# A, B and C heads of a hybrid encoder: TensorE's order written out, C keys loaded a triple ahead, value and bias loads from GpSimd's queue

## The chip, the cores and the metric

The kernel runs on one core of a Trainium2 chip. A core has five engines that work in parallel, each with its own instruction stream: PE (TensorE, matrix multiplies and transposes into PSUM), DVE (VectorE), ACT (ScalarE), POOL (GpSimd) and SP (SyncE, which here does nothing but start DMAs). An engine runs its instructions strictly in the order in which they stand, and an instruction that waits for a semaphore holds up all that stand behind it. DMAs that are started from SP, ACT or POOL stand in that engine's order too. The metric is the device time of one execution in microseconds (us).

## The reference

The program is a two-layer encoder trunk on 2048 tokens of width 1024. Four groups of attention heads run side by side on one projected input, and their outputs, each multiplied by a gate, are joined and projected back:

```python
for l in range(DEPTH):                      # DEPTH = 2
    h = _rmsnorm(x, norm_g[l])
    z = jnp.einsum('bsd,de->bse', h, w_in[l])
    (q_a, k_a, v_a, g_a, q_b, k_b, v_b, g_b,
     q_c, k_c, v_c, g_c, q_d, k_d, v_d, g_d) = jnp.split(z, offs, axis=-1)
    ...
    o_a = _dense_blocked(q_a, k_a, ...)      # A: 4 query heads, 2 key heads, all 2048 keys
    o_b = _window_sink(q_b, k_b, ...)        # B: keys within 128 of the query, with a sink logit
    o_c = _neighbourhood(q_c, k_c, v_c, rpb_c[l], sc_hd)   # C: 8 x 16 neighbours on a grid of 32 x 64, with a bias
    o_d = _diff_blocked(q_d, k_d, ...)       # D: difference of two softmaxes
    mix = jnp.concatenate([o_a * jax.nn.silu(g_a), o_b * jax.nn.silu(g_b),
                           o_c * jax.nn.silu(g_c), o_d * jax.nn.silu(g_d)], axis=-1)
    x = x + jnp.einsum('bsm,md->bsd', mix, w_out[l])
return _rmsnorm(x, final_g)
```

## The kernel before

The kernel is written in Python as a sequence of tile operations. A framework (`TileContext` with `schedule_with_timeline_sim=True`) then places each engine's instructions: it simulates the program and takes, for each engine, the operation that its simulation finds ready first, so the order in which an engine runs its work need not be that in which the code was written. Tiles come from pools with a fixed number of buffers; a new tile waits until the readers of the buffer's earlier tile are done.

A layer has four stages: the first part of the input projection (lines L319 to L323, tiles z), the D heads with the rest of the projection beside them, the phase of the A, B and C heads, and the output projection (L222, tiles y). The change lies in the third. In layer 0 it runs from about 1070 to 1692 us, in layer 1 from about 2880 to 3530 us.

The third stage is made of 96 *units* in 32 *triples*. A triple is one A unit (two query heads that share a key head, one block of 128 queries, all 2048 keys) and two small units: for the first 16 triples B units (first key head of A, `ps` 0), for the last 16 C units (second key head of A, `ps` 1). `drive` writes the work of a triple in this order:

- 12 slots. In each slot stands one *front* of the current triple: four PE transposes of probabilities into a PSUM tile PTp (L513 for A, L530 for B and C), which ACT or DVE (every third) copies out to P or PT (`evac`, L474 and L472). Behind it stands one score step of the next triple: two matmuls into S (L496), Sb (L999) or Sc (L1036), which DVE reduces to maxima while it copies them out (L497, L1001, L1037). ACT takes the exponentials (L504 for A).
- then the *backs*, the products of the probabilities with the values: 16 matmuls into O for the A unit (L519, `dense_back`), and into Obc, one PSUM tile for both small units, for B or C (L538, `small_back`). fp32 matmuls show up as two passes in the profile. Before, the backs go through their blocks downwards, and through the units of the triple from last to first.
- then the *finishes* (`fin_plain`), which run within the first three slots of the next triple: the first step copies each unit's output to an SBUF tile os (L567 to L570 for A with ACT and DVE, L572 for B and C with ACT), and POOL multiplies the gate by the reciprocal sum into gg (L543). Two slots later (`finish2`) PE transposes gg into the upper half of O or Obc (L548: O<-idr,gg, Obc<-idr,gg), DVE multiplies it by os into mix (L551) or mixc (L558), and a DMA stores that in mx. The os and gg tiles come from the pool `ov`, which has two buffers for each.

`prep(ps, t + 1)` runs when the scores of unit t start. It loads the queries (q, L963) and, in some triples, keys: `k_batch` loads a block of 512 keys of the A, B or C heads into kl (L947; pool `ql`, one buffer), transposes them on PE into kT (L98) and splits them in two terms (L954, L956) into the long key tiles kA, kB, kC. These, and the value tiles vc of the C heads, share a pool `big` of ten buffers, so that a vc tile takes the buffer of a key tile that is done. `load_vc` fills a vc tile with 6 to 8 DMAs (L940), `load_bias` a bias tile (bedge, bint) with a memset and four DMAs (L148, L152). SP starts nearly all DMAs: gates gt (L614, L616), q, kl, vc, bias, mx and the output weights wos (L254).

## Time and profile before

| | us |
|---|---|
| median of 3 runs | 3717.33 |
| lowest and highest run | 3710.25, 3719.14 |
| the profiled execution, its time | 3713.1 |
| the profiled execution, its span | 3711.3 |
| PE busy | 3516.1 (95%) |
| DVE busy | 2492.1 (67%) |
| ACT busy | 2095.2 (56%) |
| POOL busy | 944.4 (25%) |

The span is the stretch from the first to the last recorded instruction of the profiled execution; its time has 1.8 us around it. Rows of a timeline read: start in us, duration in us, engine, line, operation, output<-inputs, number of instructions that the row joins, and in brackets how long the engine had been idle and what ended that. SPq stands for the DMA starts on SP's queue, PE for matmuls, PEld for weight loads (they overlap with PE). Rows of waits read: engine, tile and line that waited <- what it waited for: us in total, times, longest. Rows of a stretch read: from:to, length, then busy time and count of PE, PEld, DVE, ACT, POOL, then the granted TensorE clock (1.00 is full speed), the busy share of the DMA engines and GB/s.

### The profile page before, as it was taken

How to read it: one execution, taken by the hardware profiler on the slowest of the kernel's cores; microseconds unless marked ns; L12 is line 12 of the kernel's file. 1: busy time of each engine (PE TensorE's matmuls, PEld its weight loads, DVE VectorE, ACT ScalarE, POOL GpSimd, SP SyncE). 2: the span in 40 equal slices, each digit the busy share in tenths (PEclk: the TensorE clock that was granted, in tenths of full speed). 3: DMA queues.
4: the chain of work that ended last, by engine and by line, in shares of the span. 5: the costliest groups of instructions: out<-in, count | busy, mean ns of one | idle time of the engine just before them, and what ended most of it. 6: DMA issues, size and time to landing. Idle time of an engine off the chain costs nothing.

```text
span 3711.3 us, 71694 instructions
## 1 busy us (share of the span) xinstructions
PE 3516.1 (95%) x25232; PEld 2967.4 (80%) x25232; DVE 2492.1 (67%) x7829; ACT 2095.2 (56%) x3961; POOL 944.4 (25%) x1604
## 2 busy tenths in 40 slices
PE   8989999999989788999999899999999897899999
PEld 8979898888957666777899798989888676677787
DVE  4377878778777665774233778787877776667733
ACT  4345656556657565772143556565666676667721
POOL 4455324533100000001034553254321000000000
PEclk9999999999999998999999999999999899999999
DMA  4532225332133323325345323252232323343243
GB/s 142 191 100 83 80 76 172 86 83 83 59 98 86 89 83 107 93 78 181 132 129 192 98 78 86 78 182 73 78 84 73 90 81 92 88 117 89 87 151 119
DMA packets 353867, 386.44 MB, mean 104 GB/s; under 512 B 58914, under 2 KB 296674, under 8 KB 348386
## 3 DMA queue, kind: packets, MB, share of 16 engines
q1 hardware_dynamic: 349186, 366.11, 33.4%
q10 hardware_dynamic: 4320, 15.73, 1.2%
q8 instruction: 200, 3.28, 0.4%
q14 instruction: 161, 1.32, 0.1%
HBM read 258.83 MB, written 122.86 MB: 103 GB/s over the span
## 4 chain that ended last, share of the span: by engine, by line
PE 76%; DVE 7%; DMA 5%; POOL 4%; ACT 3%; issue 3%; SPq 2%; POOLq 0%; DVEq 0%; ACTq 0%
PE O L519 11%; PE S L496 10%; PE PTp L513 10%; PE y L222 10%; PE z L319 9%; PE z L321 9%; PE z L323 9%; DVE P L497 3%; PE PTp L530 2%; PE Obc L538 2%; ACT P L504 2%; PE Sc L1036 2%; SPq L940 1%; DMA wst<-in_w_in_dram 1%; DVE wt L313 1%
## 5 line engine op out<-in xcount | busy, mean ns | idle before, releaser
L497 DVE TENSOR_SCALAR_CACHE_REDUCE P<-S 128x512 f32<-128x512 f32 x1536 | 1017.7, 686 | 255.6 <-PE S L496 166.2
L319 PE MATMUL z<-wt,ht 128*128 128x256 f32 (+1 forms) x3008 | 891.3, 297 | 19.8 <-POOL wt L312 10.4
L321 PE MATMUL z<-wt,ht 128*128 128x256 f32 (+1 forms) x3008 | 882.9, 294 | 2.6 <-DVE wt L313 2.6
L323 PE MATMUL z<-wt,ht 128*128 128x256 f32 (+1 forms) x3008 | 882.3, 294 | 0.0
L513 PE MATMUL PTp<-idr,P 128*128 128x128 f32 x4096 | 624.6, 278 | 19.4 <-ACT P L474 10.3
L474 ACT COPY P<-PTp 128x512 f32<-128x512 f32 x864 | 491.3, 583 | 217.1 <-PE PTp L513 210.4
L319 PEld LDWEIGHTS z<-wt,ht 128*128 128x128 f32 x3008 | 568.8, 189 | 38.8 <-POOL wt L312 12.5
L504 ACT ACTIVATE P<-P,nm 128x2048 f32<-128x2048 f32 x256 | 513.9, 2008 | 144.4 <-DVE jk L503 139.9
L321 PEld LDWEIGHTS z<-wt,ht 128*128 128x128 f32 x3008 | 569.0, 189 | 16.1 <-DVE wt L313 4.6
L513 PEld LDWEIGHTS PTp<-idr,P 128*128 128x128 f32 x4096 | 491.5, 143 | 111.0 <-issue 23.6
L323 PEld LDWEIGHTS z<-wt,ht 128*128 128x128 f32 x3008 | 569.1, 189 | 8.4 <-issue 0.8
L496 PE MATMUL S<-kA,q 128*128 128x512 f32 x1024 | 348.1, 435 | 0.3
L543 POOL TENSOR_TENSOR gg<-gt,rzh 128x128 f32<-128x128 f32 x192 | 78.8, 411 | 1016.1 <-PE O L548 578.4
L222 PE MATMUL y<-wot,ms 128*128 128x512 f32 x1440 | 332.9, 393 | 3.4 <-ACT ms L211 2.0
L222 PEld LDWEIGHTS y<-wot,ms 128*128 128x128 f32 x1440 | 271.9, 189 | 64.2 <-ACT ms L211 2.4
L720 DVE SCALAR_TENSOR_TENSOR P<-P,cf,P 128x2048 f32<-128x2048 f32 x128 | 306.4, 2394 | 2.5
L312 POOL TENSOR_SCALAR wt<-wst,g 128x256 fp32r<-128x256 f32 (+1 forms) x336 | 208.2, 631 | 390.0 <-PE z L323 290.8
L504 ACT ACTIVATE P<-P,nm,rr_a 128x2048 f32<-128x2048 f32 x128 | 268.8, 2100 | 62.6 <-DVE jk L503 61.8
L519 PE MATMUL O<-P,vA 128*64 128x256 f32 x2048 | 272.6, 392 | 0.0
L519 PE MATMUL O<-P,vd 128*64 128x256 f32 x2048 | 240.9, 388 | 1.6 <-ACT P L474 1.6
L313 DVE SCALAR_TENSOR_TENSOR wt<-wst,g,wt 128x256 fp32r<-128x256 f32 (+1 forms) x344 | 195.3, 596 | 44.2 <-POOL wt L312 40.5
L496 PE MATMUL S<-kdt,qd 128*128 128x512 f32 x512 | 214.6, 442 | 8.3 <-DVE P L497 5.8
(195 smaller groups left out, 5130.6 us busy)
## 6 DMA issues: line engine op xcount, KB each, us to landing
wst<-in_w_in_dram SPq DMA_DIRECT2D x320, 128.0 KB
qd<-qd SPq DMA_DIRECT2D x128, 128.0 KB
htd<-ht SPq DMA_DIRECT2D x16, 1024.0 KB
ht<-htd SPq DMA_DIRECT2D x16, 1024.0 KB
q<-qsA SPq DMA_DIRECT2D x128, 128.0 KB
q<-qsB SPq DMA_DIRECT2D x64, 256.0 KB
q<-qc SPq DMA_DIRECT2D x64, 256.0 KB
mload<-mx ACTq DMA_DIRECT2D x30, 512.0 KB
```

The lines of the kernel that those rows point to most:

```text
L222: PE.matmul(ys[c], lhsT=ms[:, a, kc], rhs=wts[k][:, b, c * 512:(c + 1) * 512], start=(k == 0 and i == 0), stop=(k == KD - 1 and i == 2))
L313: V.scalar_tensor_tensor(wt[:, 1, :], s, g8[:, k:k + 1], wt[:, 0, :].bitcast(F32), op0=ALU.mult, op1=ALU.subtract)
L319: PE.matmul(z, lhsT=h[:, 0, kc], rhs=wk[:, 0, :], start=(k == 0), stop=False)
L321: PE.matmul(z, lhsT=h[:, 0, kc], rhs=wk[:, 1, :], start=False, stop=False)
L323: PE.matmul(z, lhsT=h[:, 1, kc], rhs=wk[:, 0, :], start=False, stop=(k == KD - 1))
L474: A.copy(dst, src)
L496: PE.matmul(s, lhsT=q, rhs=k_ap[:, c:c + 512], start=(i == 0), stop=(i == len(q_list) - 1))
L497: V.tensor_scalar(p[:, c:c + 512], s, 1.0, None, op0=ALU.mult, op1=ALU.max, accum_out=mx[:, j:j + 1])
L504: A.activation(p, p, ACTF.Exp, bias=nm, scale=scale, accum_out=zacc)
L513: PE.transpose(tp[:, (h * 2 + a) * 128:(h * 2 + a + 1) * 128], p[:, h, j * 128:(j + 1) * 128], idn)
L519: PE.matmul(u["o"][a * 64:(a + 1) * 64, 0:256], lhsT=u["v"](0, j), rhs=u["p"][:, :, j * 128:(j + 1) * 128], start=(j >= NT - 2), stop=(j < 2))
L720: V.scalar_tensor_tensor(p0, p1, cf, p0, op0=ALU.mult, op1=ALU.add)
```

## The change

It has four parts.

1. The `drive` of the A, B and C heads stands in `tc.manual_schedule` for PE: within it PE's instructions are issued in the order in which the code is written. The other engines are still placed by the simulation.
2. The backs of a triple are written as A, first small unit, second small unit, and their blocks upwards (`fixed`; the D heads keep the downward order).
3. `k_batch` is split. `k_load` starts the DMA of the keys at one `prep`, `k_build` transposes and splits them at the next; `ql` has two buffers. The first B block is still loaded and built at once.
4. The DMAs of `load_vc` and `load_bias` are started from POOL's queue (`nc.gpsimd`): in both layers 120 for vc and 48 for bias.

Lines after the first edit move: L543 is L544 after, L548 is L549, L513 stays, L538 is L539, L940 is L941, L947 is L948, L963 is L970, L1036 is L1043.

```diff
--- before.py
+++ after.py
@@ -149,7 +149,7 @@
         for r in range(4):
             i0 = min(max(4 * rg + r - 4, 0), 24) - w0
             row = w0 + i0 - 4 * rg - r + 7
-            nc.sync.dma_start(out=dst[r * 32:r * 32 + 32, :, i0 * 40:i0 * 40 + 320],
+            nc.gpsimd.dma_start(out=dst[r * 32:r * 32 + 32, :, i0 * 40:i0 * 40 + 320],
                               in_=rep_d[l][ch][:, :, row * 40:row * 40 + 320])
 
     ht = {}
@@ -514,10 +514,11 @@
                 evac(p[:, :, c], tp.rearrange("p (h k) -> p h k", h=2), u["ev"])
 
             def dense_back(u):
-                for j in reversed(range(NT)):
+                js = range(NT) if u["fixed"] else range(NT - 1, -1, -1)
+                for n, j in enumerate(js):
                     a = j % 2
                     PE.matmul(u["o"][a * 64:(a + 1) * 64, 0:256], lhsT=u["v"](0, j), rhs=u["p"][:, :, j * 128:(j + 1) * 128],
-                              start=(j >= NT - 2), stop=(j < 2))
+                              start=(n < 2), stop=(n >= NT - 2))
 
             def small_front(u, i):
                 ws, n, kw = u["ws"], u["n"], u.get("kw", 128)
@@ -533,10 +534,10 @@
 
             def small_back(u):
                 n, kw = u["n"], u.get("kw", 128)
-                for j in reversed(range(n)):
+                for j in range(n):
                     for h in range(2):
                         PE.matmul(u["o"][h * 64:(h + 1) * 64, u["oc"]:u["oc"] + 128], lhsT=u["v"](h, j),
-                                  rhs=u["pt"][0:kw, (j * 2 + h) * 128:(j * 2 + h + 1) * 128], start=(j == n - 1), stop=(j == 0))
+                                  rhs=u["pt"][0:kw, (j * 2 + h) * 128:(j * 2 + h + 1) * 128], start=(j == 0), stop=(j == n - 1))
 
             def finish(gt, coef):
                 gg = ov.tile([128, 2, 64], F32, tag="gg", name="gg")
@@ -683,7 +684,7 @@
                     flush()
                     for u in g:
                         u["get_o"](u)
-                    for u in reversed(g):
+                    for u in g:
                         u["back"](u)
                     for u in g:
                         fins.append(u["fin"](u))
@@ -909,7 +910,7 @@
                             return kds[kv, c]
                         return f
                     units = [dict(kv=kv, t=t, k=get_kd(kv), qp=dv, s=d_scores, par=True, ns=16, nv=8, ev=0, fin=fin_d, fb=6 + kv,
-                                  p1=p1p, front=dense_front, back=dense_back, get_o=own_o,
+                                  p1=p1p, fixed=False, front=dense_front, back=dense_back, get_o=own_o,
                                   v=lambda h, j, kv=kv: vd[:, j, kv * 64:(kv + 1) * 64]) for kv in range(2) for t in range(NT)]
 
                     for u in units:
@@ -937,14 +938,20 @@
                     for j in range(nr // 3):
                         k0 = (w0 + 3 * j) * 64 + 24 * ch
                         src = bass.AP(tensor=vc_d.tensor, offset=vc_d.offset + k0 * 256, ap=[[16384, 3], [256, 40], [1, 256]])
-                        nc.sync.dma_start(out=v[0:120, ch, j, :], in_=src)
+                        nc.gpsimd.dma_start(out=v[0:120, ch, j, :], in_=src)
                 return v
 
-            def k_batch(ql, g, b):
-                c = slice(b * 512, (b + 1) * 512)
+            def k_load(ql, g, b):
+                kls = []
                 for pr in range(2 if g == "C" else 1):
                     kl = ql.tile([128, 4, 128], F32R, tag="kl", name="kl")
                     nc.sync.dma_start(out=kl.bitcast(F32), in_=ks_d[g, b][:, :, pr * 128:(pr + 1) * 128])
+                    kls.append(kl)
+                return kls
+
+            def k_build(g, b, kls):
+                c = slice(b * 512, (b + 1) * 512)
+                for pr, kl in enumerate(kls):
                     p = tps.tile([128, 512], F32, tag="t", name="kT")
                     for i in range(4):
                         transpose_raw(p[:, i * 128:(i + 1) * 128], kl[:, i, :])
@@ -1051,7 +1058,7 @@
 
             def a_unit(kv, t, q, pre):
                 return dict(kv=kv, t=t, s=a_scores, par=True, ev=EVA1 if kv else EV3, ns=8, nv=8, fin=fin_plain, fb=kv, q=q, pre=pre,
-                            front=dense_front, back=dense_back, get_o=own_o, oc=0,
+                            front=dense_front, back=dense_back, get_o=own_o, oc=0, fixed=True,
                             v=lambda h, j: vt["A"][:, j, kv * 64:(kv + 1) * 64])
 
             def pair_o(u):
@@ -1065,7 +1072,7 @@
                 return dict(kv=i, t=t, s=sc, par=False, ev=EVC if sc is c_scores else EVB, ns=ns, nv=nv, fin=fin_plain, fb=fb, q=q, pp=px, bias=bias, pre=pre,
                             front=small_front, back=small_back, get_o=pair_o, oc=128 * i, ptp=ptp)
 
-            with tc.tile_pool(name="qst", bufs=2, reuse_waits="tile") as qst, tc.tile_pool(name="ql", bufs=1, reuse_waits="tile") as ql, \
+            with tc.tile_pool(name="qst", bufs=2, reuse_waits="tile") as qst, tc.tile_pool(name="ql", bufs=2, reuse_waits="tile") as ql, \
                     tc.tile_pool(name="cb", bufs=1, reuse_waits="tile") as cb, tc.tile_pool(name="px", bufs=4, reuse_waits="tile") as px, \
                     tc.tile_pool(name="pt", bufs=2, reuse_waits="tile") as ptp, \
                     tc.tile_pool(name="ops2", bufs=1, space=PSUM, reuse_waits="tile") as ops2, \
@@ -1073,22 +1080,28 @@
                 tpool = cycle([tps, tps, tps3])
                 load_v("A")
                 kt["B"] = [big.tile([128, S], F32R, tag="b", name=f"kB{i}") for i in range(2)]
-                k_batch(ql, "B", 0)
+                k_build("B", 0, k_load(ql, "B", 0))
                 load_v("B")
+                loaded = []
                 bint = [None, cb.tile([128, 4, 480], F32, name="bint1")]
                 cc_ = {}
                 cm = {"pool": cb}
                 qq = {}
 
                 def prep(ps, t):
+                    while loaded:
+                        k_build(*loaded.pop(0))
                     if t < NT:
                         g = "BC"[ps]
+                        nk = None
                         if ps == 0 and t % 4 == 2 and t < 14:
-                            k_batch(ql, "B", t // 4 + 1)
+                            nk = "B", t // 4 + 1
                         if ps == 0 and t == 4:
                             kt["A"].append(big.tile([128, S], F32R, tag="b", name="kA1"))
                         if ps == 0 and 4 <= t < 8:
-                            k_batch(ql, "A", t - 4)
+                            loaded.append(("A", t - 4, k_load(ql, "A", t - 4)))
+                        if nk:
+                            loaded.append((*nk, k_load(ql, *nk)))
                         if ps == 1 and t == 2:
                             bint[0] = big2.tile([128, 4, 512], F32, tag="b", name="bint0")[:, :, 0:480]
                             load_bias(l, bint[0], 3, 0)
@@ -1096,7 +1109,7 @@
                             load_bias(l, bint[1], 3, 1)
                             kt["C"] = [big.tile([128, S], F32R, tag="b", name=f"kC{i}") for i in range(4)]
                         if ps == 0 and t >= 12:
-                            k_batch(ql, "C", t - 12)
+                            loaded.append(("C", t - 12, k_load(ql, "C", t - 12)))
                         qq["A", ps, t] = q_batch(qst, "A", t, 2 * ps, 2)
                         qq[g, ps, t] = q_batch(qst, g, t, 0, 4)
                     elif ps == 0:
@@ -1131,7 +1144,8 @@
                             if k == MS0:
                                 ms_first.append(load_split(mx_d[0].rearrange("p a b -> p (a b)"), dv, "qd"))
                             wo_tiles.append(load_split(w_out[l, k * 128:(k + 1) * 128, :], dv, "qd"))
-                drive([units[i:i + 3] for i in range(0, len(units), 3)], GAP3, iter(()), 0, ex3)
+                with tc.manual_schedule(engines={mybir.EngineType.PE}):
+                    drive([units[i:i + 3] for i in range(0, len(units), 3)], GAP3, iter(()), 0, ex3)
 
         dvx.close()
         prev_mx = mx_d
```

On PE, in the third B triple of layer 1, the finishing transposes (O<-idr,gg of the A unit, Obc<-idr,gg of the two B units) stood like this among scores S and Sb and fronts PTp before:

```order
L548 MATMUL O<-idr,gg 128x128
L496 MATMUL S<-kA_35899,q 128x512 x2
L513 MATMUL PTp<-idr,P 128x128 x4
L496 MATMUL S<-kA_35899,q 128x512 x4
L513 MATMUL PTp<-idr,P 128x128 x4
L548 MATMUL Obc<-idr,gg 128x128
L513 MATMUL PTp<-idr,P 128x128 x8
L496 MATMUL S<-kA_35899,q 128x512 x4
L999 MATMUL Sb<-kB_38469,q 128x384
L1000 MATMUL Sb<-kB_38469,q 128x384
L513 MATMUL PTp<-idr,P 128x128 x4
L548 MATMUL Obc<-idr,gg 128x128
```

and so after:

```order
L496 MATMUL S<-kA_35902,q 128x512 x2
L513 MATMUL PTp<-idr,P 128x128 x4
L496 MATMUL S<-kA_35902,q 128x512 x2
L513 MATMUL PTp<-idr,P 128x128 x4
L549 MATMUL O<-idr,gg 128x128
L549 MATMUL Obc<-idr,gg 128x128 x2
L496 MATMUL S<-kA_35902,q 128x512 x2
L513 MATMUL PTp<-idr,P 128x128 x4
```

The three transposes that lay apart, with four score steps and more between the first and the last, stand next to each other, and fronts and scores alternate one by one.

On POOL, in the phase of layer 0, the gates gg stood alone but for the memsets of the bias tiles before:

```order
L543 TENSOR_TENSOR gg<-gt,rzh 128x128 x47
L148 MEMSET bedge 128x1440
L148 MEMSET bint_18895 128x4x480
L543 TENSOR_TENSOR gg<-gt,rzh 128x128 x3
L148 MEMSET bedge 128x1440
```

and after they stand with the vc loads among them (gg x33 is eleven triples):

```order
L544 TENSOR_TENSOR gg<-gt,rzh 128x128 x33
L941 DMA vc<-vc_211 120x1x256 x14
L544 TENSOR_TENSOR gg<-gt,rzh 128x128 x11
L941 DMA vc<-vc_211 120x1x256 x22
L544 TENSOR_TENSOR gg<-gt,rzh 128x128
```

22 of them stand between the second and the third gg of the fifteenth triple. Later in the phase, runs of 8, 8 and 6 stand between the second and the third gg of three C triples.

On SP, around the load of the second block of C keys (kl<-ksC_1) in layer 0, before:

```order
L963 DMA q<-qsB_13_162 64x1024
L616 DMA gt<-gsB_11_206 128x128
L552 DMA mx_9_230<-mix 128x128
L963 DMA q<-qsB_13_162 64x1024
L940 DMA vc<-vc_211 120x1x256 x11
L947 DMA kl<-ksC_1_174 128x4x128
L616 DMA gt<-gsA_12_191 128x128
```

and after:

```order
L553 DMA mx_9_230<-mix 128x128
L617 DMA gt<-gsB_11_206 128x128
L970 DMA q<-qsA_14_147 64x512 x2
L970 DMA q<-qsB_13_162 64x1024 x2
L948 DMA kl<-ksC_1_174 128x4x128 x2
L617 DMA gt<-gsA_12_191 128x128
```

The eleven vc loads that stood directly ahead of the keys are gone from SP, and both halves of the block are loaded one behind the other.

## The prediction

> **What bounds the kernel now.** I read the page first, then the busy time of each engine in the two A/B/C phases, then TensorE's waits there, and last the timelines around the waits. PE is the bound of the whole program:

> ```profile
> span 3711.3 us, 71694 instructions
> PE 3516.1 (95%) x25232; PEld 2967.4 (80%) x25232; DVE 2492.1 (67%) x7829; ACT 2095.2 (56%) x3961; POOL 944.4 (25%) x1604
> ```

> The profiled execution took 3713.1 us, 4.2 below the median 3717.33 and inside the three runs' 3710.25 to 3719.14. 0.3%, about 11 us, is what a measurement of this kernel can tell from no change. The change touches only the phase of the A, B and C heads, which is the stretch from 1070 to 1692 us in layer 0 and from 2880 to 3530 us in layer 1. These four rows give each engine's busy time there, and the granted clock:

> ```profile
> 1070.00:1370.00 300.00, 269.46 (x2022) 203.64 (x2020) 214.35 (x813) 203.55 (x441) 19.73 (x48) 0.95 0.30 82
> 1370.00:1692.00 322.00, 297.70 (x2278) 222.35 (x2277) 215.19 (x746) 209.17 (x412) 26.60 (x55) 0.96 0.33 94
> 2880.00:3190.00 310.00, 274.80 (x1992) 203.79 (x1991) 226.07 (x831) 210.09 (x433) 20.22 (x48) 0.95 0.31 85
> 3190.00:3530.00 340.00, 323.77 (x2488) 241.59 (x2488) 233.84 (x819) 228.50 (x459) 28.91 (x61) 0.98 0.35 99
> ```

> PE is busy 1165.7 of 1272 us: no more than 106 us can come from filling its gaps. The largest wait of PE, first of layer 0, then of layer 1 (in total, times, longest):

> ```profile
> PE kT L98 <- DMA kl<-ksC: 19.4, 3, 18.1
> ...
> PE kT L98 <- DMA kl<-ksC: 18.8, 3, 17.9
> ```

> So 38 us of the gaps are two stalls on C keys, and they have a visible cause: on SP's queue the load of these keys (L947) stands behind eleven vc loads.

> ```profile
> 1271.55 19.29 SPq L940 DMA_DIRECT2D vc<-vc  x11
> 1290.95 1.58 SPq L947 DMA_DIRECT2D kl<-ksC  x1
> 1299.41 0.75 PE L98 MATMUL kT<-idr,kl 128*128 128x128 f32 x4 [18.13 <-DMA kl<-ksC]
> ```

> **Part 1: written order and early keys, the gain.** I measure a triple by the start of its first finishing transpose (O<-idr,gg): 32 in each layer, 31 intervals.

> ```profile
> 1113.59 0.27 PE L548 MATMUL O<-idr,gg 128*128 128x128 f32 x1
> 1180.19 0.27 PE L548 MATMUL O<-idr,gg 128*128 128x128 f32 x1
> 1195.70 0.27 PE L548 MATMUL O<-idr,gg 128*128 128x128 f32 x1
> 1318.59 0.27 PE L548 MATMUL O<-idr,gg 128*128 128x128 f32 x1
> 1338.06 0.27 PE L548 MATMUL O<-idr,gg 128*128 128x128 f32 x1
> 1501.74 0.27 PE L548 MATMUL O<-idr,gg 128*128 128x128 f32 x1
> 1518.63 0.27 PE L548 MATMUL O<-idr,gg 128*128 128x128 f32 x1
> 1679.62 0.27 PE L548 MATMUL O<-idr,gg 128*128 128x128 f32 x1
> 1692.08 0.30 PE L548 MATMUL O<-idr,gg 128*128 128x128 f32 x1 [1.28 <-DVE os L570]
> 2959.54 0.27 PE L548 MATMUL O<-idr,gg 128*128 128x128 f32 x1
> 3524.41 0.30 PE L548 MATMUL O<-idr,gg 128*128 128x128 f32 x1 [0.70 <-DVE os L570]
> ```

> The 31 intervals last 578.5 us in layer 0 and 564.9 in layer 1. An undisturbed B triple takes 15.51 (1180.19 to 1195.70), a C triple 16.89 (1501.74 to 1518.63, with no gap on PE), a B triple that also builds C keys 19.47, the last interval 12.46. In written order every triple has the same plain alternation, so I give each its undisturbed length: 15 x 15.51 + 15 x 16.89 + 12.46 = 498.5, plus 4 x 3.96 for C keys, plus 7 other key builds at 0.4 (half of the 0.75 us above, where the clock was 0.50) = 517.1 per layer. The gain is 61.4 + 47.8 = 109.2 us. It holds the two key stalls, the small waits and the piecemeal order of the late C triples; taking the backs as A, B, B and in ascending order, the second ql buffer and the loads a triple ahead are in it and cost nothing more (the same matmuls; SP has fewer DMAs ahead of the keys). If small waits of the ACT kind survive, up to 20 of it fails.

> **Part 2: the finishing chain, the loss.** The three finishing transposes of a triple stand apart in the order before, with scores of later slots between. In written order they are neighbours. Each hangs on the last: the third os copy on ACT writes the buffer that mix of the first transpose frees on DVE; Obc's first transpose writes the tile that this copy reads; Obc's second needs the mixc that follows the first. Before, the same chain runs with cover:

> ```profile
> 1501.77 0.71 PE L496 MATMUL S<-kA,q 128*128 128x512 f32 x2
> 1502.09 0.40 POOL L543 TENSOR_TENSOR gg<-gt,rzh 128x128 f32<-128x128 f32 x1 [9.99 <-DMA q<-qsA]
> 1502.84 0.29 DVE L551 TENSOR_TENSOR mix<-O,os 128x128 f32<-128x128 f32 x1
> 1503.43 0.27 ACT L572 COPY os<-Obc 128x128 f32<-128x128 f32 x1
> 1505.46 0.27 PE L548 MATMUL Obc<-idr,gg 128*128 128x128 f32 x1
> 1506.27 0.29 DVE L558 TENSOR_TENSOR mixc<-Obc,os 128x128 f32<-128x128 f32 x1
> 1508.24 0.27 PE L548 MATMUL Obc<-idr,gg 128*128 128x128 f32 x1
> ```

> It took 6.5 us, 1501.74 to 1508.24, and none of it was idle on PE. Now PE stands still for it, since it issues in order. Its hand-overs, where nothing else is in the way, are short:

> ```profile
> 1693.18 0.29 DVE L551 TENSOR_TENSOR mix<-O,os 128x128 f32<-128x128 f32 x1
> 1693.51 0.27 ACT L572 COPY os<-Obc 128x128 f32<-128x128 f32 x1 [0.92 <-DVE mix L551]
> 1323.08 0.56 ACT L474 COPY P<-PTp 128x512 f32<-128x512 f32 x1
> 1323.70 0.66 PE L530 MATMUL PTp<-idr,Pb 128*128 128x128 f32 x4 [1.13 <-ACT P L474]
> ```

> From the first transpose at 0: mix starts at 1.10 (1502.84 - 1501.74; DVE has the same score and probability copies ahead of it) and ends at 1.39, the copy starts 0.04 later and ends at 1.70, PE 0.06 after that at 1.76; 0.35 to the next engine (POOL's gg 1502.09 after 1501.74) gives mixc at 2.11 to 2.40, and the third transpose at 2.46. A transpose alone delays the next matmul by 0.03 (1501.77), so the net loss is 2.46 - 2 x 0.03 = 2.40 us. The ends: 1.0 if the chain were half covered, which the waits as built do not allow but a fast DVE would approach (without the 0.75 us in which DVE is behind it is 1.65), and 3.0 if another ACT copy (0.56) stands in the way. I take 2.40, since the DVE queue ahead of mix is that of the rows. 62 triples x 2.40 = 148.8 us. Behind the waiting transpose stand the scores S, and DVE, ACT and the next triple wait for them.

> **Part 3: the clock.** A stall of this size also slows what follows it:

> ```profile
> 1100.00:1103.40 3.40, 1.53 (x12) 1.00 0.78 189
> 1103.40:1106.90 3.50, 3.50 (x18) 0.51 0.06 14
> ```

> PE was busy 1.53 of 3.40 us, and the next 3.5 us ran at 0.51. That costs half of 3.4, 1.7 us. A stall that idles PE for some 1.9 us leaves a 3.4 us window under half busy only when nearly all of it falls into that window, for (3.4 - 2.4)/3.4 = 0.3 of the triples. 62/3 x 1.7 = 35 us; the ends are 0 and 105 (every triple). [...]

> **Part 4: vc and bias loads on POOL.** 120 vc and 48 bias DMAs leave SP for POOL's queue, where gg (L543) runs, and gg feeds the chain. In the new order 22 vc loads stand ahead of the third gg of one B triple of each layer, and 8, 8 and 6 ahead of that of three C triples. What one costs POOL no row shows; the nearest are SP's own:

> ```profile
> L940 SPq DMA_DIRECT2D vc<-vc x120: 681/750/2484, 1266.4 to 3356.8; - x120
> 1516.45 4.90 SPq L940 DMA_DIRECT2D vc<-vc x5
> 1512.71 1.95 PE L519 MATMUL O<-P,vA 128*64 128x256 f32 x16
> 1514.48 1.92 PE L538 MATMUL Obc<-PT,vc 120*64 120x128 f32 x32
> 1516.33 0.66 PE L513 MATMUL PTp<-idr,P 128*128 128x128 f32 x4
> ```

> The cover: the 8 wait for the last Obc of the old buffer, which ends at 1516.33, 2.30 before the first transpose; with the chain's 2.46 that is 4.76 us. The 22 wait first for the last S on the old A keys, which ends four score slots, O's back and a B back earlier: slots of 0.92 (two and a half of them in the 2.30), a back of two times 1.77 (1512.71 to 1514.48) and 24 of the 32 passes that take 1.85 (1514.48 to 1516.33): 3.7 + 3.5 + 1.4 + 4.8 = 13.4 us. At the 0.98 us of the run of five (4.90/5) the stalls are 22 x 0.98 + 0.40 (the gg itself) - 13.4 = 8.6, twice 8 x 0.98 + 0.40 - 4.76 = 3.5, and 1.5: 17.1 per layer, 34.2 in all. At the median 0.75 it is 14; at the 1.75 of the run of eleven 102; at the longest, 2.48, 166; at a gg's 0.40 nothing. I take 0.98, the price with the queue not choked. The 14 vc loads ahead of another triple's first gg have a whole triple to run in (14 x 0.98 = 13.7 of 15.51), and the bias loads, 4 at a time, fit in the cover. Moving them off SP gains nothing beyond part 1.

> [...]

> **Sum.** 3713.1 - 109.2 + 148.8 + 35.1 + 34.2 = 3822.0 us, 2.9% above the profiled execution and 2.8% above the median.

> **Rivals.**
> - *Faster.* The chain costs less than 109.2/62 = 1.76 us a triple, nothing else grows. For it: 1.65 if DVE reaches mix at once. Against it: in the steady triple DVE is not there at once. At 1.0 us, no clock loss and 14 for POOL: 3713 - 109 + 62 + 14 = 3680.
> - *About unchanged.* 1.65 a triple and no clock loss: 3713 - 109 + 102 + 14 = 3720.
> - *Worse: DVE's work holds POOL's issue up.* Each vc load then costs POOL 1.75 to 2.48 us (the run of eleven, the longest row) and PE waits for gg: 102 to 166 in place of 34, 3890 to 3954. For it: gg and 22 loads in one queue, and DVE is busy 70% of this phase (889 of 1272 us in the four rows). [...]
> - *The change doesn't do what it says.* The key stalls come back, because the loads still stand on SP's one queue behind loads that wait for buffers: 38 us of the gain fail, 3860. Against: no vc load stands ahead of a kl load on SP any more.

> **Chances.** The sum's case 0.56 (its own range 3755 to 3885, from chains of 1.8 to 2.7 us and a clock loss of 0 to 60), faster 0.23, about unchanged 0.07, worse 0.10, stalls back 0.04. The range, 3680 to 3925, cuts a third of the faster case and half of the worse. Faster by over 0.3%: 0.23; within: 0.07; slower: 0.70.

> **What would show it.** Right: in the new trace, Obc's transposes wait on ACT os and on DVE mixc in nearly each triple, together about 2 us; kT waits on kl are gone; intervals of 17.9 for B and 19.3 for C triples; a granted clock under 0.95 in these phases; gg late behind vc loads in four triples a layer. Wrong: no such waits and B triples near 15.5, or POOL's DMA rows under 0.5 us with the clock at 1.00.

## The result, and the profile after

The changed kernel takes 3816.02 us (median of 4 runs, 3813.22 to 3819.26) against 3718.23 (4 runs, 3710.25 to 3726.55): the ratio is 1.0263, 95% interval 1.0239 to 1.0287, so it is 2.6% slower. The forecast was 3822, with a range of 3680 to 3925.

The head of the page after, span and PE:

```profile
span 3811.3 us, 71858 instructions
PE 3522.4 (92%) x25232; PEld 3021.1 (79%) x25232; DVE 2521.7 (66%) x7829; ACT 2097.8 (55%) x3961; POOL 1056.8 (28%) x1772
```

PE is as busy as before (3516.1) and the span is 100 us longer, so at first sight all of the loss is idle time of PE. The busy time by stretch says where it is. The stretches run from the first O<-idr,gg of a layer to the last; these are the two of before (columns as in the prediction):

```profile
1113.59:1692.08 578.49, 529.67 (x4059) 399.51 (x4057) 401.14 (x1445) 385.99 (x795) 43.38 (x97) 0.96 0.32 91
2959.54:3524.41 564.87, 525.99 (x4058) 395.78 (x4057) 401.00 (x1444) 385.88 (x795) 43.26 (x97) 0.98 0.33 93
```

and these the two of after:

```profile
1116.00:1743.41 627.41, 538.26 (x4088) 427.90 (x4087) 420.49 (x1457) 390.11 (x800) 94.84 (x173) 0.93 0.33 84
3001.11:3624.88 623.77, 536.60 (x4087) 427.51 (x4086) 420.87 (x1456) 390.06 (x799) 94.91 (x173) 0.93 0.33 84
```

The phases grew by 48.9 and 58.9 us, 107.8 together; the stage between them got 9.8 shorter. PE's idle time went from 87.7 to 176.3 us, its busy time up by 19, at a lower clock. What PE waits for in the two phases after, layer 0 first:

```profile
PE Obc L549 <- ACT os L573: 50.1, 31, 2.8
PE Obc L549 <- POOL gg L544: 20.1, 29, 2.8
PE O L549 <- DVE os L571: 6.2, 2, 5.1
...
PE Obc L549 <- ACT os L573: 48.0, 31, 2.5
PE Obc L549 <- POOL gg L544: 27.8, 29, 11.1
```

The four rows of Obc are 146 us in 120 waits, all at the second and third finishing transpose. No wait for kl is left. One steady C triple, in the timelines of PE, DVE, ACT and POOL, shows the chain:

```profile
1562.66 0.27 PE L549 MATMUL O<-idr,gg 128*128 128x128 f32 x1
1563.75 0.29 DVE L552 TENSOR_TENSOR mix<-O,os 128x128 f32<-128x128 f32 x1
1564.08 0.27 ACT L573 COPY os<-Obc 128x128 f32<-128x128 f32 x1 [1.53 <-DVE mix L552]
1564.49 0.30 PE L549 MATMUL Obc<-idr,gg 128*128 128x128 f32 x1 [1.56 <-ACT os L573]
1564.83 0.29 DVE L559 TENSOR_TENSOR mixc<-Obc,os 128x128 f32<-128x128 f32 x1 [0.78 <-PE Obc L549]
1564.87 0.40 POOL L544 TENSOR_TENSOR gg<-gt,rzh 128x128 f32<-128x128 f32 x1 [1.46 <-PE Obc L549]
1565.26 0.30 PE L549 MATMUL Obc<-idr,gg 128*128 128x128 f32 x1 [0.47 <-POOL gg L544]
1565.32 0.71 PE L496 MATMUL S<-kA,q 128*128 128x512 f32 x2
```

From the first transpose: mix at 1.09, the copy at 1.42, the second transpose at 1.83, mixc at 2.17, the third transpose at 2.60, the next score at 2.66. The next such transpose comes at 1581.60, an interval of 18.94 us.

The view puts the last 0.47 us down to gg, but it was mixc that the third transpose waited for. This gg ends at 1565.27, after the transpose has started (1565.26); mixc ends at 1565.12, 0.14 before it, the same 0.14 that lie between the end of the os copy (1564.35) and the second transpose, and so it is in all 54 triples without a late gg. The transpose's own gg was made at 1563.01, in the buffer that the first transpose freed; the one of 1564.87 is that of the next triple's A unit. So of the rows above that name gg, 0.47 us a triple is the hand-over of mixc (of mix in B triples), and only what goes beyond it is a late gg. In eight triples the wait is longer: 2.78, 2.79, 1.99 and 0.62 us in layer 0, 11.07, 2.05, 2.00 and 0.80 in layer 1, in the four triples of a layer that have vc loads ahead of their third gg.

The clock, in three stretches of 3.4 us behind the triple before this one:

```profile
1541.20:1544.60 3.40, 1.45 (x10) 0.92 (x8) 2.33 (x7) 0.85 (x2) 3.40 (x6) 0.98 0.52 106
1544.60:1548.00 3.40, 3.17 (x12) 2.57 (x13) 1.09 (x4) 0.59 (x1) 0.92 (x3) 0.52 0.86 190
1548.00:1551.40 3.40, 3.40 (x25) 2.86 (x24) 3.35 (x11) 2.99 (x4) 0.00 (x0) 1.00 0.28 86
```

A stretch with PE busy 1.45 of 3.40 us is followed by one at half clock, and that triple takes 20.58 us (1542.08 to 1562.66). In the clock's records there are 40 stretches at half clock in the two phases, 31 of 3.41 us and 9 two or four times as long, 181 us in all; before there were 7, 72 us in all. PE is busy 156.9 us in them, against 30.5. Half of that is lost: 78 us against 15.

The record shows how idle PE has to be. Of the 314 windows of 3.41 us at full clock in these phases, all 40 that a slow one followed had PE busy for less than 47.9% by the profile's records, and all others for more. A slow stretch ended after the first window with PE busy for 86.0% or more.

And POOL, in the timelines of POOL and PE, in the triple of layer 1 with 22 vc loads:

```profile
3263.92 5.65 POOL L941 DMA_DIRECT2D vc<-vc  x8 [6.40 <-PE S L496]
3285.50 0.78 POOL L544 TENSOR_TENSOR gg<-gt,rzh 128x128 f32<-128x128 f32 x2
3285.98 0.48 PE L549 MATMUL Obc<-idr,gg 128*128 128x128 f32 x1 [11.07 <-POOL gg L544]
```

and the vc line's instructions grouped (shortest, median, longest ns, and the time to landing):

```profile
L941 POOL DMA_DIRECT2D vc<-vc x120: 690/710/777, 1302.0 to 3426.6; - x120
...
DMA to landing us min/median/max: 4.7/6.0/10.7
```

A load costs POOL 0.71 us (median), and the run of 22 keeps the gg waiting from 3263.92 to 3285.50.

### The profile page after: what moved, and what is told of

It is laid out like the page before. It is cut to its first block, busy times and chain, and to the rows that moved or that the text cites. A ratio compares the mean times of both kernels' runs of the same rounds, so it can differ in the third digit from the quotient of the medians.

```text
span 3811.3 us, 71858 instructions
## 1 busy us (share of the span) xinstructions
PE 3522.4 (92%) x25232; PEld 3021.1 (79%) x25232; DVE 2521.7 (66%) x7829; ACT 2097.8 (55%) x3961; POOL 1056.8 (28%) x1772
## 5 line engine op out<-in xcount | busy, mean ns | idle before, releaser
L319 PE MATMUL z<-wt,ht 128*128 128x256 f32 (+1 forms) x3008 | 891.2, 297 | 18.6 <-POOL wt L312 9.4
L474 ACT COPY P<-PTp 128x512 f32<-128x512 f32 x864 | 491.4, 583 | 420.8 <-PE PTp L513 415.6
L513 PE MATMUL PTp<-idr,P 128*128 128x128 f32 x4096 | 664.5, 288 | 30.3 <-DVE kC L964 10.0
L513 PEld LDWEIGHTS PTp<-idr,P 128*128 128x128 f32 x4096 | 528.0, 150 | 144.2 <-issue 46.1
L319 PEld LDWEIGHTS z<-wt,ht 128*128 128x128 f32 x3008 | 568.6, 189 | 37.5 <-POOL wt L312 11.2
L496 PE MATMUL S<-kA,q 128*128 128x512 f32 x1024 | 407.2, 484 | 1.1 <-DVE P L497 1.1
L544 POOL TENSOR_TENSOR gg<-gt,rzh 128x128 f32<-128x128 f32 x192 | 80.0, 422 | 924.2 <-PE O L549 595.7
L504 ACT ACTIVATE P<-P,nm,rr_a 128x2048 f32<-128x2048 f32 x128 | 268.8, 2100 | 31.2 <-DVE jk L503 30.5
L520 PE MATMUL O<-P,vA 128*64 128x256 f32 x2048 | 235.1, 382 | 0.0
L496 PE MATMUL S<-kdt,qd 128*128 128x512 f32 x512 | 215.1, 444 | 12.4 <-DVE P L497 10.1
```

The costliest lines, as they stand in the source:

```text
L319: PE.matmul(z, lhsT=h[:, 0, kc], rhs=wk[:, 0, :], start=(k == 0), stop=False)
L474: A.copy(dst, src)
L496: PE.matmul(s, lhsT=q, rhs=k_ap[:, c:c + 512], start=(i == 0), stop=(i == len(q_list) - 1))
L504: A.activation(p, p, ACTF.Exp, bias=nm, scale=scale, accum_out=zacc)
L513: PE.transpose(tp[:, (h * 2 + a) * 128:(h * 2 + a + 1) * 128], p[:, h, j * 128:(j + 1) * 128], idn)
L520: PE.matmul(u["o"][a * 64:(a + 1) * 64, 0:256], lhsT=u["v"](0, j), rhs=u["p"][:, :, j * 128:(j + 1) * 128], start=(n < 2), stop=(n >= NT - 2))
```

## The experiments

The kernel before, run again beside these, has medians of 3720 to 3721 us. Each kernel starts from the changed one unless it says otherwise; `...` marks where code is left out.

**Transposes apart.** The small units wait two and four slots longer before `finish2`; the order on PE is still the written one.

```diff
-                yield
-                yield
+                for _ in range(u.get("late", 2)):
+                    yield
                 finish2(gg, os, ...)
...
-                        ... oc=128 * i, ptp=ptp)
+                        ... oc=128 * i, ptp=ptp, late=4 + 2 * i)
```

> The changed kernel with the finishing transposes of the two small units two and four slots later, so that they stand apart again in the written order. Theory (the finishing chain): PE's waits at the Obc transposes, 147 us in the two phases of the changed kernel, fall below 20, of its 40 stretches at half clock at most 12 stay, and the time falls by about 126 + 55 us to 3635 us (3610 to 3670). Rival (written order is slow by itself, or the loads on POOL are the cost): the waits move to other rows (S on DVE, Obc on a late gg) and the time stays over 3750 us.

3626.53 us, ratio 0.9748 (0.9733 to 0.9763): 190 us less than the changed kernel and faster than before. The waits of Obc's transposes on os fell to 4.7 and 4.2 us, one late gg of 10.0 us stayed in layer 1, and 3 stretches of half clock (24 us) are left of 40 (181 us). With the transposes apart the whole loss is gone: written order and loads on POOL are not slow by themselves.

**Four buffers instead.** The transposes stay neighbours.

```diff
-                gg = ov.tile([128, 2, 64], F32, tag="gg", name="gg")
+                gg = ov.tile([128, 2, 64], F32, tag="gg", name="gg", bufs=4)
...
-                os = ov.tile([128, 128], F32, tag="os", name="os")
+                os = ov.tile([128, 128], F32, tag="os", name="os", bufs=4)
```

> The changed kernel with four buffers in place of two for os and gg, the transposes left next to each other. Theory: the wait of the first Obc transpose on ACT's os copy disappears, but the second still waits for mixc of the first, which DVE reaches at about 1.4 us: a stall of some 1.75 us in place of 2.60, so 53 us of waits and a part of the clock loss go: about 3735 us (3710 to 3765). Rival (the two buffers are the whole cause): as with the transposes apart, 3640 us. Rival (buffers do nothing): 3816 us.

3687.74 us, ratio 0.9914 (0.9895 to 0.9933): faster than the range that I expected. PE's waits in layer 0:

```profile
PE Obc L549 <- DVE mixc L559: 23.8, 15, 2.3
PE Obc L549 <- DVE mix L552: 18.6, 16, 2.5
```

and the phase of layer 0 by stretch:

```profile
1114.80:1677.70 562.90, 501.55 (x4088) 401.65 (x4086) 412.57 (x1456) 387.14 (x798) 95.29 (x175) 0.98 0.39 95
```

The wait on os is gone and one on mix or mixc has come, (23.8 + 18.6)/31 = 1.4 us a triple; most C triples take 18.1 us. Here the view names mixc itself at the third transpose. The chain shortened as worked out. What I had wrong was the clock: with 1.4 us of idle PE a triple 5 stretches of half clock are left in both layers together, with the 2.03 us (1.56 + 0.47) of the changed kernel there are 40.

**Loads back on SP.**

```diff
-                        nc.gpsimd.dma_start(out=v[0:120, ch, j, :], in_=src)
+                        nc.sync.dma_start(out=v[0:120, ch, j, :], in_=src)
... (load_bias likewise)
```

> The changed kernel with the vc and bias loads back on SP's queue. Theory: the gg that stand behind vc loads on POOL come in time, about 22 us of waits and a few us of clock go, and the key stalls of 18 us do not return, since the keys are now loaded ahead: 3790 us (3770 to 3800). Rival (the loads on POOL were what removed the key stalls): kT waits on kl again for 15 to 40 us: 3820 to 3850 us.

3870.23 us, ratio 1.0410 (1.0392 to 1.0429). The theory fell, and the rival had the direction without the size (3820 to 3850) or the place: no kT waits on kl. A wait of PE in layer 0:

```profile
PE S L496 <- DVE P L497: 41.7, 3, 17.4
```

What ended the idle time of DVE ahead of mix (us, times), from the group of its line in this kernel:

```profile
  DMA mx<-mix: 108.1, 25
```

and in the changed one:

```profile
  DMA mx<-mix: 25.6, 24
```

One of the three, in the timelines of SP, DVE and PE:

```profile
1319.03 4.83 SPq L941 DMA_DIRECT2D vc<-vc  x3
1323.97 4.62 SPq L948 DMA_DIRECT2D kl<-ksC  x2
1330.16 0.87 SPq L553 DMA_DIRECT2D mx<-mix  x2
1335.09 0.29 DVE L552 TENSOR_TENSOR mix<-Obc,os 128x128 f32<-128x128 f32 x1 [14.08 <-DMA mx<-mix]
1336.04 1.22 PE L496 MATMUL S<-kA,q 128*128 128x512 f32 x2 [11.88 <-DVE P L497]
```

SP's queue holds the store of mix behind the vc loads and the loads that follow them; DVE's next mix needs the buffer that this store reads, scores stand behind mix on DVE, and PE's S waits for DVE three times a layer. Beside it the waits that the view puts down to gg fell to 14.7 us in each layer, 31 times the hand-over of 0.47. The price of the loads on POOL in the changed kernel is what stood above that: 20.1 + 27.8 in 58 waits, less 58 x 0.474, 20.4 us.

**Loads on SP, transposes apart.** The edits of the first and the third run together.

> Transposes apart as in the first run, and the vc and bias loads back on SP's queue. Theory: on SP the stores of mix stand behind vc loads, DVE's next mix waits for its buffer and PE's S for DVE, three times a layer (42 us a layer in the run with loads on SP); it does not hang on the finishing chain, so it costs the same here: 3627 + 60 to 85 us, about 3700 us (3685 to 3715). Rival (the cost came from the chain, which left DVE no slack): 3620 to 3640 us.

3688.86 us, ratio 0.9909 (0.9892 to 0.9926), inside the theory's range and 62 more than with the loads on POOL. PE waits for DVE 37 us in each layer (16.0, 11.4 and 10.1 in layer 0). So the step that moves the loads off SP is worth 62 us in this kernel, and 54 (3870 - 3816) in the changed one.

**Keys ahead alone.** From the kernel before: the `k_load` and `k_build` part and the second kl buffer, nothing else.

> The kernel before with one part of the change alone: keys loaded a triple ahead, two buffers for kl; PE placed by the simulation, loads on SP, backs downwards as before. Theory: the two key stalls of 18 us go, the rest stays: 3718 - 36 = 3682 us (3670 to 3700). Rival (the third key block still stands behind eleven vc loads on SP, and a triple ahead is not enough): kT waits of 10 us or more stay, 3700 to 3720 us.

3717.57 us (10 runs), ratio 0.9994 (0.9984 to 1.0003): no change. The kT waits are gone, and these stand in their place (layer 0):

```profile
PE Obc L539 <- DVE mix L552: 15.4, 1, 15.4
PE PTp L531 <- DVE P L472: 12.0, 2, 11.6
PE S L496 <- DVE P L497: 10.8, 1, 10.8
```

Behind the wait on DVE P stands again a mix that waits 11.1 us for DMA mx<-mix. The stall belonged to the vc loads on SP; the keys were only what was late first.

**PE placed by the simulation.** The changed kernel without `manual_schedule`.

> The changed kernel without the written order: PE is placed by the simulation again, with keys loaded a triple ahead, the loads on POOL and the backs as in the changed kernel. Theory: the finishing transposes stand apart, so no chain stall; the two key stalls of 18 us are gone: 3718 - 38 = 3680 us (3665 to 3700). Rival (the loads on POOL cost in any order): gg behind vc loads takes the place of the key stalls, 3700 to 3740 us.

3741.85 us, ratio 1.0060 (1.0045 to 1.0075): 62 us over the theory, and its rival names the wrong cause too: no wait on gg is left, and all waits of PE in the phase of layer 0 are under 9 us together. That phase:

```profile
1113.60:1706.10 592.50, 583.92 (x4075) 394.65 (x4074) 412.55 (x1449) 391.16 (x797) 93.88 (x173) 0.99 0.35 89
```

The O passes of two C triples, grouped by line, in this kernel:

```profile
L520 PE MATMUL O<-P,vA 128*64 128x256 f32 x64 | 11.2, 393 | 0.0
```

in the kernel before:

```profile
L519 PE MATMUL O<-P,vA 128*64 128x256 f32 x64 | 7.8, 385 | 0.0
```

and in the one with the transposes apart:

```profile
L520 PE MATMUL O<-P,vA 128*64 128x256 f32 x64 | 7.3, 382 | 0.0
```

PE is busy 583.9 of 592.5 us, at a clock of 0.99, with the same matmuls. In these two triples the back of O stands in seven pieces of 1 to 12 passes each among 128-wide work, and 64 passes take 11.2 us in place of 7.3. "Busy" here is no measure of work. That the pieces cost time was only a reading so far; the next run tests it.

**The back of O in four pieces.** With the transposes apart, `dense_back` of the A unit is issued four matmuls at a time between front and score of the last four slots.

```diff
+                            if a.get("fixed") and u is not a:
+                                ...
+                                    a["chunk"] = slice(4 * (i - 9), 4 * (i - 8))
+                                    a["back"](a)
```

> Transposes apart, and the back of the A unit cut in four pieces of four matmuls that stand between the fronts and scores of the last four slots, the same matmuls in all. Theory (a piece of back between 128-column work costs PE busy time that no wait shows): in the kernel whose PE was placed by the simulation the O passes took 5.6 us a triple in pieces, here 3.65 in one run; four pieces then cost 1.6 to 2.2 us a triple, 100 to 135 us over 62 triples: about 3740 us (3710 to 3765), with the O rows at 5 us or more a triple and no new wait. Rival (pieces are free, the simulation's order is slow for another reason): 3620 to 3640 us.

3701.08 us, ratio 0.9947 (0.9932 to 0.9961): 75 us more for the same matmuls in pieces, which excludes the rival, though it is less than I expected. The O passes of two C triples:

```profile
L521 PE MATMUL O<-P,vA 128*64 128x256 f32 x64 | 8.7, 392 | 0.0
```

No wait of PE grew by more than 7 us in a layer; most C triples take 18.15 in place of 16.79, 1.36 us more, about 0.34 us a piece. Half of that, 0.7 us, stands in the O rows. The timeline shows where the rest is:

```profile
1474.64 0.60 PE L513 MATMUL PTp<-idr,P 128*128 128x128 f32 x4
1475.00 0.72 PE L496 MATMUL S<-kA,q 128*128 128x512 f32 x2
1475.55 0.60 PE L532 MATMUL PTp<-idr,Pc 128*120 128x128 f32 x4
1476.08 1.08 PE L521 MATMUL O<-P,vA 128*64 128x256 f32 x8
1477.10 0.71 PE L1053 MATMUL Sc<-kC,q 128*128 128x480 f32 x2
```

A front that a score follows takes 0.36 us to the next start (1474.64 to 1475.00), one that a piece of O follows 0.53 (1475.55 to 1476.08): 0.17 us ahead of each of the four pieces, 0.7 us again.

**Apart and four buffers.** The edits of the first two runs.

> Transposes apart and four buffers for os and gg. Theory: the chain is already covered by the distance, so the buffers have only the remaining waits on os (9 us) and the one late gg of 10 us to take: 3612 us (3600 to 3625). Rival (the distance covers all of it): 3627 us as without the buffers.

3612.58 us, ratio 0.9712 (0.9698 to 0.9727): the best of all, 2.9% faster than before. Its phase of layer 0:

```profile
1116.33:1641.93 525.60, 498.87 (x4087) 399.27 (x4086) 404.56 (x1455) 388.38 (x799) 96.73 (x175) 0.99 0.41 101
```

Most C triples take 16.5 to 16.7 us. In the kernel before most take 16.9 us with the back of O in two pieces and 17.1 to 18.9 with O in four to six; in the changed one they take 18.1 to 23.4.

**Four mix buffers, bias loads on SP**, on top of that.

> Transposes apart, four buffers for os, gg and also for mix, vc loads on POOL and the 48 bias loads back on SP. Theory: with four mix buffers DVE waits no longer for the stores of mix, and the bias loads no longer stand behind a gg on POOL (one wait of 3.6 us for bedge): some 5 to 10 us less than 3613: 3605 us (3595 to 3612). Rival (bias loads on SP bring back a part of SP's queue stalls): 3620 to 3640 us.

3615.52 us, ratio 0.9718 (0.9702 to 0.9734): the theory's gain did not come, and the kernel can't be told from the one it came from. Once the vc loads are off SP, more mix buffers and the bias loads on SP give nothing together; each alone was not run.

**The order alone.** From the kernel before: `manual_schedule` and the order of the backs, nothing else.

> The kernel before with the written order and the order of the backs alone: keys loaded and built at once, one kl buffer, vc and bias loads on SP. Theory: the chain stall and its clock loss as in the changed kernel, plus SP's queue stalls as in the run with the loads on SP (3870), where the key stalls of 18 us come at the same places and so add little: 3880 us (3860 to 3910). Rival (early keys and loads on POOL cost more than they give): 3780 to 3816 us.

3890.35 us, ratio 1.0459 (1.0444 to 1.0475), as the theory had it. Early keys and the loads on POOL are worth 74 us to the changed kernel: 20 for the early keys (3890 - 3870, both with the loads on SP) and 54 for the loads.

## Why the prediction came out, and which of its steps did not

The sum was 3713.1 - 109 + 149 + 35 + 34. The kernel with the transposes apart and four buffers has all of the change but the chain, so it splits the result: 3718 - 3613 = 105 us of gain, and 3816 - 3613 = 203 of loss, where the prediction had 109 and 218. (Its four buffers are an extra that is worth 14 us; without them the split is 92 and 190.)

- *What bounds the kernel.* It was right that PE does. The 106 us of gaps were no limit, and the prediction's own 109, which counts the piecemeal order of the late C triples, already passes them: in the best kernel PE is busy 997.6 us in the two phases against 1055.7 before, and only 9 of these 58 are clock. The rest is the order of the same matmuls. Pieces of O are one part of it, as the run with four pieces shows; how large a part was not measured.
- *Part 1, the gain.* 109 was right in size, but its account was not. It took the key stalls as won by early keys; keys ahead alone gave nothing, since the next thing behind the vc loads on SP, the store of mix, is late by as much. Part 4's sentence that moving the loads off SP "gains nothing beyond part 1" is the step that failed: it gains 62 us. I had found the queue and its eleven loads, and did not ask who else stands behind them. On the other side I priced a triple by rows of before in which the back of O stands in two pieces (16.89); with the transposes apart and O in one piece it takes 16.79, and with four buffers 16.55.
- *Part 2, the chain.* The mechanism is shown, each hand-over of it. Against the best kernel a steady C triple without clock loss takes 18.94 - 16.55 = 2.39 us more; 2.40 was the forecast. Mix, copy and second transpose came at 1.09, 1.42 and 1.83 (forecast 1.10, 1.43 and 1.76), mixc and the third transpose at 2.17 and 2.60 (2.11 and 2.46); most of the difference is that PE starts 0.14 us after the engine that it waits for and not 0.06. Not every triple is like this one: in the 54 triples without a late gg the two transposes wait 1.4 to 2.9 us together, and the chain's waits are some 126 us in all (146 less the 20 of the late gg's).
- *Part 3, the clock.* That a stall slows what follows it was right, the size half of what it is: 35 for about 72 us (78 less the 6 of the best kernel). No run of before shows this term: that the clock goes by windows of 3.4 us, that half busy is the border and that the stall falls into such a window in 0.3 of the triples was my estimate from one stretch (1.53 of 3.40 us busy, then 0.51). I gave a third of the 62 triples a slow stretch of 3.4 us, 21 of them; there were 40 stretches with a length of 53 times 3.41 us, all behind windows with PE busy for less than 47.9%. In the clock's records of the changed kernel every stretch but the last is a whole multiple of 3.41 us long, at half or at full rate. In the C triples most of them start 20.5 us after one another, six times 3.41, which is close to the length of a slow triple, so that the next stall may fall at the same place of its window. That was not tested. PE need not be idle for all of a window: a stretch with 1.45 us busy of 3.40 was still followed by one at 0.52.
- *Part 4, POOL.* About 20 us for 34. The four late gg's a layer came where they were forecast. A load costs 0.71 and not 0.98, and yet the run of 22 took 21.6 us, what 0.98 gives, since POOL waited 3.9 us between them for earlier vc loads to land. PE waited 11.1 us for the gg behind it in layer 1. In layer 0 it was only 2.8, because PE had stood still in that triple before: DVE waited 9.5 us for a small load (snk). The runs of 8 cost 1.5 to 2.3 us each (forecast 3.5), the runs of 6 under 0.4 (forecast 1.5). The rival by which DVE's work holds POOL's issue up is excluded for this kernel: 690 to 777 ns for all 120 loads with DVE 66% busy.
- *The rivals.* The faster one needed a chain under 1.76 us. Its mechanism exists: with four buffers a C triple takes 18.10 us, 1.55 more than in the best kernel, and the kernel is 0.9% faster than before.
- *The range.* The ends of the sum's own case, 3755 and 3885, do not follow from what it names: chains of 1.8 and 2.7 us with clock losses of 0 and 60 give 3750 and 3865.

That the total came within 6 us is in part luck. The losses close like this: in the two phases the changed kernel is 200 us longer than the best one, 77 of it busy time of PE (72 are clock) and 123 idle time. The idle time is the 146 us at the transposes, 20 of them late gg's, less 23, because the stalls cover other idle time: beside the chain PE is idle 30 us in the changed kernel (176 less 146) and 54 in the best one (1051.3 less 997.6). The prediction put the clock 37 us too low and POOL 14 too high, and it had no term for the cover.

## What to carry to other kernels

When an order is written by hand for one engine, look at every group of short instructions that becomes neighbours and follow what each needs from the other engines: here three transposes in a row cost about 2.4 us each time, and moving two of them by two and four slots turned a loss of 2.6% into a gain of 2.5%. When a load stands in a queue behind others, moving that load alone may only show the next one behind (keys ahead alone: ratio 0.9994): move what blocks (the loads off SP: 62 us with the transposes apart). A PE that is busy without a gap can still lose time to the order of its work: compare the time of the same matmuls in one piece and in pieces, here 7.3 us for 64 passes in one piece a triple against 11.2 in seven. And where a view names what ended a wait, compare the end of that instruction with the start of the one that waited: here gg was named, and mixc was meant.
